# Both feed-forward down stages with seven half products, and operand sums made in the up stages

## The chip, the core and the metric

One core of a Trainium2 chip runs the whole layer. The metric is the device time of one execution in microseconds (us). TensorE (PE) multiplies, VectorE (DVE) and ScalarE (ACT) work on tiles, GpSimd (POOL) does tiny root computations and issues DMAs, SyncE (SP) issues most DMAs.

## What is computed

One layer for 2048 tokens of width 1024: a norm, a combined projection, attention and a time mixing, then a merge with `w_out`, a residual, and a feed-forward block with a residual:

```
m = sigmoid(gA) * (yA @ proj_a) + sigmoid(gB) * (yB @ proj_b)
x = x + RMSNorm_post(m @ w_out)
x = x + RMSNorm_post2(relu(RMSNorm_pre2(x) @ w_up)^2 @ w_down)
```

`w_up` is 1024x4096, `w_down` 4096x1024, all in float32. Each factor is split into a high and a low part (`split`, L72: a cast by ACT, a subtraction by DVE), and a product is three matmuls (`mm3`, L77).

## The kernel before

The tokens are four groups `g` of 512. For each group the kernel runs the time mixing, the attention and `phase_merge` (L987), whose last part is the output projection: 192 matmuls `ps_o`, after which ACT copies the result into the tiles `o` and they are stored to `od`. Under the projection of groups 1 and 2, `after` (L1070) runs the residual of the group before, one 128-token tile after the other (`residual_steps`, L1028): load `o` and `x`, mean square on ACT, root on POOL, two DVE steps that give the new `x` (stored to `x1`), a second mean square and root, one DVE step with the gain, eight transposes on PE (`ps_ht`), two copies `hf` on ACT and their stores to `ht`.

The feed-forward block works on two halves of two groups each: up, down, up, down. An up stage (`phase_up`, L1125) has 16 blocks `i`. A block multiplies a 256-column piece of `w_up` by the two groups with seven products of half size in place of eight, for which sums of the four quarters of the tokens (`t1` to `t4`, `b22`) and of the weights (`s1` to `s4`) are wanted. The first two products of a block need no sums; those of blocks 0 to 7 are made ahead, in the two PSUM banks of pool `pd`, and meanwhile `operands` makes the `t` tiles ready: it loads sums that `combinations` (L1095) has made earlier and stored in `td`, and splits them. The result goes through relu and square (`hidden`, L1184). ACT's copy is called `z`, DVE's first addition `r`.

The first down stage (`phase_down`, L1255) is plain: 32 blocks of 128 rows of `w_down`, two at a time, added into `u`. Beside it run the residuals of groups 2 and 3 (`residuals`, L1063), the `combinations` of the second half and the first operand of the second up stage (`first_half`). Its closing steps (`final`) norm `u`, add the residual and store `out`. The second down stage (`phase_down_sums`, L1327) takes 8 of the 32 blocks plainly and the other 24 in three batches of seven half products. For that the second up stage also stores sums of its hidden tiles (`differences`, L1201, on DVE, stores by POOL); there the square is made by ACT, in the first up stage by DVE with stores by POOL.

A recording layer decides where each instruction stands in its engine's order; each engine takes its own in that order.

## Time and profile before

| what | us |
|---|---|
| median of 3 runs | 3340.6 (3338.98 to 3341.16) |
| profiled execution | 3337.64 |
| its span, first to last instruction | 3335.9 |
| output projection of group 3 | 1987.33 to 2034.26 |
| first up stage | 2034.26 to 2340.18 |
| first down stage | 2340.18 to 2700.22 |
| second up stage | 2700.22 to 3009.26 |
| second down stage, to the last matmul | 3009.26 to 3326.22 |

The times of the stages are read in windows from the span's start. A row of windows gives each engine's busy time with its instruction count, then the clock that was granted to PE (1.00 is full), the DMA share and GB/s. Rows of a wait give the sum, the count and the longest.

### The profile page before, as it was taken

Reading aid. Unit: us, or ns where it says so; the run is one execution under the profiler, and the core shown is the slowest. Engines: PE = TensorE matmul, PEld = TensorE weight load, DVE = VectorE, ACT = ScalarE, POOL = GpSimd, SP = SyncE. Lnnn points to the kernel's source line nnn. Section 1 sums busy time; section 2 is a strip of 40 time slices with the busy share of each in tenths; the row PEclk is TensorE's granted clock in tenths of the full one; section 3 lists DMA queues with packets and bytes.
Section 4 is the critical chain, followed back from the end, with each engine's and each line's share of the span. In section 5 each row is a group of like instructions: output and inputs, shape, how many; then the busy total and the mean of one; then the engine's idle time right before and its main releaser. Section 6 shows DMA issues by size and latency. Waiting matters only on the chain. (4 is left out here: it accounts for less than half of the span.)

```text
span 3335.9 us, 49381 instructions
## 1 busy us (share of the span) xinstructions
PE 3244.5 (97%) x19089; PEld 2608.4 (78%) x19089; DVE 2284.0 (68%) x3814; ACT 1463.2 (44%) x2331; POOL 382.7 (11%) x732
## 2 busy tenths in 40 slices
PE   7999999999999999999999999999999999999998
PEld 6777787777777777777777777888888878888887
DVE  6774656765665774565774675877877787776788
ACT  4434634444644444644434644333431254454432
POOL 2210002111012210012210000111200011100000
PEclk9999999999999999999999999999999999999999
DMA  5224343125263224354224256434756364554444
GB/s 157 80 89 147 98 145 120 61 90 182 91 236 129 69 86 168 106 205 151 83 83 152 87 206 237 131 120 142 268 177 202 106 242 162 169 171 153 141 162 133
DMA packets 166099, 478.43 MB, mean 143 GB/s; under 512 B 17564, under 2 KB 34144, under 8 KB 163176
## 3 DMA queue, kind: packets, MB, share of 16 engines
q1 hardware_dynamic: 110004, 361.97, 32.9%
q0 software_dynamic: 18688, 63.98, 5.0%
q10 hardware_dynamic: 37172, 49.32, 4.1%
q8 instruction: 151, 2.47, 0.3%
q14 instruction: 84, 0.69, 0.1%
HBM read 355.64 MB, written 122.71 MB: 143 GB/s over the span
## 5 line engine op out<-in xcount | busy, mean ns | idle before, releaser
L83 PE MATMUL psd<-hh,whi 128*128 128x512 f32 x1344 | 542.5, 404 | 2.3 <-DVE QA L835 2.3
L83 PE MATMUL psd<-hl,whi 128*128 128x512 f32 x1344 | 539.3, 401 | 0.0
L83 PE MATMUL psd<-hh,wlo 128*128 128x512 f32 x1344 | 536.5, 399 | 0.0
L74 ACT CAST whi<-wraw 128x1024 fp32r<-128x1024 f32 x232 | 243.7, 1050 | 532.7 <-PE psd L83 421.9
L83 PE MATMUL ps_dn<-fop 128*128 128x512 f32 x1920 | 439.7, 390 | 2.1 <-DVE u L1291 1.5
L75 DVE TENSOR_TENSOR wlo<-wraw,whi 128x1024 fp32r<-128x1024 f32 x232 | 283.1, 1220 | 208.9 <-ACT whi L74 188.1
L83 PEld LDWEIGHTS ps_dn<-fop 128*128 128x128 f32 x1920 | 359.4, 188 | 78.6 <-DVE u L1291 2.3
L83 PEld LDWEIGHTS psd<-hh,whi 128*128 128x128 f32 x1344 | 256.1, 191 | 57.5 <-issue 3.4
L83 PEld LDWEIGHTS psd<-hh,wlo 128*128 128x128 f32 x1344 | 255.8, 190 | 54.1 <-issue 3.5
L83 PEld LDWEIGHTS psd<-hl,whi 128*128 128x128 f32 x1344 | 255.8, 190 | 50.8 <-issue 2.1
L83 PE MATMUL ps_dn<-fop,fop 128*128 128x512 f32 x1008 | 228.6, 389 | 0.0
L83 PEld LDWEIGHTS ps_dn<-fop,fop 128*128 128x128 f32 x1008 | 189.3, 188 | 39.2
L1291 DVE TENSOR_TENSOR u<-u,ps_dn 128x512 f32<-128x512 f32 x240 | 160.6, 683 | 54.3 <-PE ps_dn L83 53.8
L895 DVE CUSTOM_DVE_ANT_0 sc<-bias,ps_s 128x640 f32<-128x640 f32 (+4 forms) x128 | 94.1, 735 | 54.6 <-PE ps_s L889 50.6
L74 ACT CAST fop<-wdraw 128x1024 fp32r<-128x1024 f32 x40 | 41.9, 1047 | 191.8 <-DVE u L1291 88.7
L900 ACT ACTIVATE sc<-sc,mn 128x640 f32<-128x640 f32 (+4 forms) x128 | 97.8, 764 | 35.2 <-DVE mn L895 30.1
L74 ACT CAST s12h<-s 128x1024 fp32r<-128x1024 f32 x32 | 33.7, 1054 | 169.5 <-PE ps_u L83 169.5
L1019 PE MATMUL ps_o<-whi,mh 128*128 128x512 f32 x256 | 101.9, 398 | 1.9 <-ACT o L1025 1.9
L83 PE MATMUL ps_p<-yh,whi 128*128 128x512 f32 x256 | 102.1, 399 | 0.7 <-DVE th L985 0.7
L1019 PE MATMUL ps_o<-wlo,mh 128*128 128x512 f32 x256 | 101.8, 397 | 0.7 <-DVE wlo L75 0.7
L83 PE MATMUL ps_p<-yh,wlo 128*128 128x512 f32 x256 | 102.1, 399 | 0.0
L83 PE MATMUL ps_p<-yl,whi 128*128 128x512 f32 x256 | 101.5, 396 | 0.0
(378 smaller groups left out, 6741.8 us busy)
## 6 DMA issues: line engine op xcount, KB each, us to landing
wraw<-in_w_in_dram SPq DMA_DIRECT2D x168, 512.0 KB, 3.7
wraw<-in_w_up_dram SPq DMA_DIRECT2D x80, 512.0 KB, 4.5
ar<-sd SPq DMA_DIRECT2D x21, 1024.0 KB, 4.8
wdraw<-in_w_down_dram SPq DMA_DIRECT2D x40, 512.0 KB, 4.0
araw<-ad SPq DMA_DIRECT2D x40, 512.0 KB, 4.0
gd<-gate ACTq DMA_DIRECT2D x64, 256.0 KB, 2.3
wraw<-in_w_out_dram SPq DMA_DIRECT2D x32, 512.0 KB, 3.7
ad<-r POOLq DMA_DIRECT2D x64, 256.0 KB, 2.4
```

Of the source, the lines that this page charges most:

```text
L74: self.nc.scalar.copy(hi, src)
L75: self.nc.vector.tensor_tensor(lo, src, hi.bitcast(F32), ALU.subtract)
L83: mm = nc.tensor.matmul(ps, l, r, start=start and n == 0, stop=stop and n == last).ins
L895: nc.vector.tensor_tensor_reduce(sc[:, 0:n], bias[:, s0:640], pss[:, c0 : c0 + n], 1.0, 3.0e38, ALU.add, ALU.min, mn,)
L900: nc.scalar.activation(sc[:, 0:n], sc[:, 0:n], AF.Exp, scale=-1.0, bias=mn, accum_out=sm)
L1019: nc.tensor.matmul(ps[t], l[:, k, ts], r[:, k % 2], start=k == 0 and j == 0, stop=k == KB - 1 and j == 2)
L1291: nc.vector.tensor_tensor(u[t][:, ns], u[t][:, ns], ps, ALU.add)
```

## The change

- `phase_down_sums` becomes `phase_down` and serves both halves; the plain stage, `combinations`, `residuals` and `td` are gone. The first up stage makes the sums of its hidden tiles as the second does.
- `operands` loads the four quarters of the tokens from `ht` into free slots of the two 16 KB `z` tiles, in two passes; each pass makes four sums on DVE and then five splits. The second pass is loaded by POOL's queue into the same slots.
- The residual of group 2 moves under the output projection of group 3; that of group 3 follows it, from the tiles `o` without a trip to memory, beside the first products of the first up stage.
- A closing step of a tile (`final`) is queued behind the first half of the next tile. In the first half `out` is stored by POOL. Beside these steps, the weights of the first two blocks of the second up stage are loaded and split, and its first operand too (`nxt`).

```
-    def phase_merge(self, g, o, between, early=iter(())):
+    def phase_merge(self, g, o, between, pt, tp):
...
             advance(between)
+            if g == self.NG - 1:
+                rp = e(tc.tile_pool(name="mgr", bufs=2, reuse_waits="tile"))
+                res = [self.residual_steps(g, rp, pt, *self.gs, t, o[t]) for t in range(GT)]
+                for i in range(GT + 2):
+                    for t in (i - 2, i - 1, i):
+                        if 0 <= t < GT:
+                            advance(res[t], 1)
...
-        if 0 < g < 3:
-            gs = self.gains(sp, 3)
-            res = [self.residual_steps(g - 1, self.late, pt, *gs, t) for t in range(GT)]
+        if g > 0:
+            self.gs = self.gains(sp, 3 if g + 1 < self.NG else 2)
+            res = [self.residual_steps(g - 1, self.late, pt, *self.gs, t) for t in range(GT)]
...
             def operands():
-                td, g1 = self.td[half], self.ht[2 * half + 1]
-                for n, src in (
-                    ("t2", td[:, 3]), ("t3", td[:, 1]), ("t1", td[:, 0]), ("b22", g1[:, hi4]), ("t4", td[:, 2])
-                ):
-                    h, l = T[n]
-                    for k in (0, 2):
-                        ks = slice(k, k + 2)
-                        nc.sync.dma_start(l[:, ks].bitcast(F32), src[:, ks])
-                        self.split_here(h[:, ks], l[:, ks])
+                g0, g1 = self.ht[2 * half], self.ht[2 * half + 1]
+                t1, t3, b22, t4 = (slots[:, n : n + 2] for n in range(0, early, 2))
+                t2 = z[:, early - 2 : early]
+                for k in (0, 2):
+                    ks = slice(k, k + 2)
+                    for t, src in ((t1, g0[:, lo4]), (t3, g1[:, lo4]), (b22, g1[:, hi4]), (t4, g0[:, hi4])):
+                        (nc.gpsimd if k else nc.sync).dma_start(t, src[:, ks])
+                    for o, x, y in ((t1, t3, t1), (t2, b22, t1), (t3, b22, t3), (t4, t4, t2)):
+                        nc.vector.tensor_tensor(o, x, y, ALU.subtract)
+                    for n, src in (("t2", t2), *((("b22", b22), ("t4", t4), ("t3", t3)) if half else (("t3", t3), ("b22", b22), ("t4", t4))), ("t1", t1)):
+                        self.split(*(x[:, ks] for x in T[n]), src)
                         yield
...
             def summed(i):
-                return sums and FIRST <= i < FIRST + BATCHES * XB
+                return FIRST <= i < FIRST + BATCHES * XB
...
-                if not sums:
-                    nc.vector.tensor_tensor(out, out, out, ALU.mult)
-                    nc.gpsimd.dma_start(self.ad[fb][:, th], out)
-                    return
                 nc.scalar.activation(out, out, AF.Square)
...
             for i in range(early):
-                A11, A12 = parts(load(2 * i), ("a1", "s12", "s3")[i % 3], KB)
+                A11, A12 = made.pop(i, None) or self.up_first(i, load, parts)
...
-                for n, queue in enumerate((nc.sync, nc.scalar)):
+                for n, queue in enumerate((nc.gpsimd, nc.gpsimd) if follow else (nc.sync, nc.scalar)):
...
-                        keep(y[th][:, t, n * H : (n + 1) * H], ps, False)
+                        kept = keep(y[th][:, t, n * H : (n + 1) * H], ps, False)
                         halve(th, t, n, gt, scaled, ssq)
-                    final(th, t, fp, scaled, ssq)
+                        if n == 0 and at:
+                            with tc.issue_after(kept):
+                                final(*done)
+                            advance(beside, 1)
+                    done = th, t, fp, scaled, ssq
+            final(*done)
...
+            def nxt(loaded):
+                bp = bpool(ahead, "b1", side="right")
+                self.sp = bpool(ahead, "ops1", side="right")
+                load, parts = self.up_raw(rp), self.up_parts(self.sp)
+                for i in range(2):
+                    self.made[i] = self.up_first(i, load, parts)
+                return self.first_half(2, bp, loaded)
...
-            self.phase_up(0, zp, rp, cb, pn, 8)
-            self.phase_down(0, zp, rp, cb, pn, beside)
-            self.phase_up(1, zp, rp, cb, pn, 8, True)
-            self.phase_down_sums(1, zp, bp, rp, cb, pn)
+                with ExitStack() as u:
+                    self.phase_up(0, zp, rp, cb, pn, bpool(u, "ops", side="right"), 8, {})
+                self.phase_down(0, zp, bp, rp, cb, pn, nxt)
+            self.phase_up(1, zp, rp, cb, pn, self.sp, 8, self.made)
+            ahead.close()
+            self.phase_down(1, zp, bpool(ctx, "b2"), rp, cb, pn)
```

PE, start of the first down stage, before (`fop` are split blocks, `o_prev` normed tiles of a residual):

```order
L83 MATMUL ps_u<-t4h,s3l 128x512
L83 MATMUL ps_dn<-fop 128x512 x82
L1054 MATMUL ps_ht<-ident,o_prev 128x128 x8
L83 MATMUL ps_dn<-fop 128x512 x25
L1054 MATMUL ps_ht<-ident,o_prev 128x128 x8
```

PE at the same place after the change:

```order
L83 MATMUL ps_u<-t4h,s3l 128x512
L83 MATMUL ps_dn<-fop 128x512 x48
L83 MATMUL ps_dn<-fop_22026 128x512 x48
L83 MATMUL ps_dn<-fop_22115 128x512 x3
```

PE among the early products of the first up stage after the change (`o_18802` and `o_18803` are tiles 2 and 3 of group 3):

```order
L83 MATMUL ps_u<-bh,s3l 128x512
L1060 MATMUL ps_ht<-ident,o_18802 128x128 x8
L83 MATMUL ps_u<-bh,s3h 128x512
L83 MATMUL ps_u<-bl,s3h 128x512
...
L1060 MATMUL ps_ht<-ident,o_18803 128x128 x8
```

The transposes have left the first down stage; those of group 3 stand among the early products of the first up stage.

DVE, start of the first up stage, before (`r` takes a product from PSUM, the others are low parts of splits):

```order
L1189 TENSOR_TENSOR r<-z,ps_u 128x512
L75 TENSOR_TENSOR a1l<-wraw,a1h 128x1024
L1192 TENSOR_TENSOR r<-r 128x512
L1114 TENSOR_TENSOR t2l<-t2l,t2h 128x1024
L1189 TENSOR_TENSOR r<-z,ps_u 128x512
L75 TENSOR_TENSOR s12l<-wraw,s12h 128x1024
L1192 TENSOR_TENSOR r<-r 128x512
L1114 TENSOR_TENSOR t2l<-t2l,t2h 128x1024
L1114 TENSOR_TENSOR t3l<-t3l,t3h 128x1024
L1189 TENSOR_TENSOR r<-z,ps_u 128x512
```

DVE there after the change, from the last residual to the first pass's splits:

```order
L1046 SCALAR_TENSOR_TENSOR o_18804<-o_18804,rs_p,g_post_mix 128x1024
L1047 TENSOR_TENSOR xr<-xr,o_18804 128x1024
L1182 TENSOR_TENSOR r<-z,ps_u 128x512
L1054 SCALAR_TENSOR_TENSOR o_18804<-xr,rs_r,g_pre_ffn 128x1024
L1182 TENSOR_TENSOR r<-z,ps_u 128x512
L1214 TENSOR_TENSOR s_19947<-wraw 128x512
L75 TENSOR_TENSOR a1l<-wraw,a1h 128x1024
L75 TENSOR_TENSOR t2l<-z,t2h 128x1024
L75 TENSOR_TENSOR t3l<-slots,t3h 128x1024
L75 TENSOR_TENSOR b22l<-slots,b22h 128x1024
L75 TENSOR_TENSOR t4l<-slots,t4h 128x1024
```

DVE a little later, the second pass up to the first full block (`slots` and `z` on the left are sums, `r` belongs to blocks 6 and 7):

```order
L1155 TENSOR_TENSOR slots<-slots 128x1024
L75 TENSOR_TENSOR s4l<-s_19948,s4h 128x512
L1155 TENSOR_TENSOR z<-slots 128x1024
L1155 TENSOR_TENSOR slots<-slots 128x1024
L1155 TENSOR_TENSOR slots<-slots,z 128x1024
L75 TENSOR_TENSOR t2l<-z,t2h 128x1024
L75 TENSOR_TENSOR t3l<-slots,t3h 128x1024
L75 TENSOR_TENSOR t4l<-slots,t4h 128x1024
L1182 TENSOR_TENSOR r<-z,ps_u 128x512
L75 TENSOR_TENSOR t1l<-slots,t1h 128x1024
L1182 TENSOR_TENSOR r<-z,ps_u 128x512
L75 TENSOR_TENSOR s12l<-s_19947,s12h 128x1024
```

Where one `r` stood behind two or three splits, the `r` of blocks 3 and 4 now stand behind residual steps and those of blocks 6 and 7 behind the sums and splits of the second pass.

## The prediction

> **What bounds the kernel now.** I read the page's table of busy times first, then the windows of the stages, the two groups of the down stages' matmuls and TensorE's waits in each window. PE is TensorE, DVE VectorE, ACT ScalarE.

> ```profile
> PE 3244.5 (97%) x19089; PEld 2608.4 (78%) x19089; DVE 2284.0 (68%) x3814; ACT 1463.2 (44%) x2331; POOL 382.7 (11%) x732
> core 0: us, PE busy (x) PEld busy (x) DVE busy (x) ACT busy (x) POOL busy (x), PEclk, DMA share, GB/s
> 1475.80:1532.50 56.70, 53.15 (x258) 42.47 (x257) 33.65 (x32) 30.48 (x48) 11.78 (x26) 1.00 0.69 230
> 1987.33:2034.26 46.93, 44.76 (x194) 35.73 (x192) 23.43 (x23) 18.43 (x22) 0.71 (x1) 1.00 0.64 239
> 2034.26:2340.18 305.92, 304.96 (x1346) 252.17 (x1344) 227.38 (x313) 116.37 (x156) 33.71 (x63) 1.00 0.45 151
> 2340.18:2700.22 360.04, 357.85 (x1607) 295.73 (x1606) 288.55 (x377) 102.95 (x145) 37.05 (x73) 1.00 0.57 188
> 2700.22:3009.26 309.04, 305.12 (x1339) 250.76 (x1339) 232.98 (x315) 159.31 (x225) 30.25 (x54) 1.00 0.55 189
> 3009.26:3326.22 316.96, 316.41 (x1393) 260.92 (x1391) 243.49 (x291) 119.05 (x155) 6.74 (x21) 1.00 0.43 147
> ```

> The rows are the output projection of group 2's merge, that of group 3, then up, down, up, down of the two halves; what remains to 3335.9 is the tail. PE is busy 97% of the span and nearly all of every stage: time goes where matmuls go, and a stall has to be added to that. The first down stage takes 360.04 us, the second, which already works with seven products, 316.96.

> ```profile
> L83 PE MATMUL ps_dn<-fop 128*128 128x512 f32 x1920 | 439.7, 390 | 2.1 <-DVE u L1291 1.5
> L83 PE MATMUL ps_dn<-fop,fop 128*128 128x512 f32 x1008 | 228.6, 389 | 0.0
> ```

> One 128x512 matmul occupies PE for 439.7/1920 = 0.229 us (228.6/1008 = 0.227; the mean of 390 ns overlaps its neighbour). Up stages have 1344 of them. The 1339 of the second up window tell that five already ran in the down window ahead of it (5 x 0.229 = 1.1 us).

> **The change part by part.** First down stage. Plain, it has 32 blocks x 8 x 2 x 3 = 1536 matmuls; with sums 8 blocks x 48 + 3 x 7 x 48 = 1392. So 144 go, 33.0 us at 0.229. Its 64 transposes for the residuals of groups 2 and 3 and their waits go too. The whole is read at once from the twin: 360.04 - 1.1 - 316.96 = **42.0 us less**. DVE is no new bound there: 243.49 of 316.96 us in the twin, and the closing steps get seven more split subtractions (two ahead of the seam, four of the first operand, one late), some 8 us, in a last stretch that PE fills for 192 x 0.229 = 44 us; I count that covered, 0 to 3 us.

> Residuals of group 2 move under group 3's output projection. Group 2's projection in the first window does the same work for group 1, and another 32 transposes besides.

> ```profile
> PE ps_ht L1054 <- DVE o_prev L1048: 3.3, 4, 1.1
> ```

> In that window PE waits 3.3 us for the four tiles. 56.70 - 192 x 0.229 - 3.3 = 9.4 us for 64 transposes, so 4.7 for 32. Without those of the norm the stage takes 52.0, against 46.93 now: **+5.1**, up to 7 if the small waits of today's window stay.

> Residuals of group 3 and all operand sums move to the start of the first up stage. This is the part to work out. Today the first full block there starts at 2078.9, 44.6 us after the projection:

> ```profile
> L83 PE MATMUL ps_u<-t2h,s12h x128: 389/389/501, 2078.9 to 2997.7; 128*128 128x512 f32 x128
> 2048.29 1.22 DVE L1114 TENSOR_TENSOR t2l<-t2l,t2h 128x1024 fp32r<-128x1024 f32 x1
> 2049.42 1.22 DVE L1114 TENSOR_TENSOR t3l<-t3l,t3h 128x1024 fp32r<-128x1024 f32 x1
> 2059.50 0.68 DVE L1192 TENSOR_TENSOR r<-r 128x512 f32<-128x512 f32 x1
> 2060.10 1.22 DVE L1114 TENSOR_TENSOR t4l<-t4l,t4h 128x1024 fp32r<-128x1024 f32 x1
> 2047.02 0.63 ACT L1190 ACTIVATE r<-r 128x512 f32<-128x512 f32 x1
> 2047.55 1.04 ACT L1113 CAST t3h<-t3l 128x1024 fp32r<-128x1024 f32 x1
> 2048.49 0.58 ACT L1213 COPY z<-ps_u 128x512 f32<-128x512 f32 x1
> L1040 DVE SCALAR_TENSOR_TENSOR o_prev<-o_prev,rs_p,g_post_mix x16: 1273/1284/1289, 972.8 to 2464.8; 128x1024 f32<-128x1024 f32 x16
> L1038 ACT ACTIVATE sqo<-o_prev x16: 1052/1059/1062, 970.4 to 2460.8; 128x1024 f32<-128x1024 f32 x16
> L130 POOL TENSOR_TENSOR rs_r<-rs_v,nhalf x64: 549/558/1519, 9.4 to 3330.2; 128x1 f32<-128x1 f32 x64
> L133 POOL TENSOR_SCALAR rs_p<-rs_r x16: 226/229/1023, 972.5 to 2463.0; 128x1 f32<-128x1 f32 x16
> L1057 ACTq DMA_DIRECT2D ht<-hf x32: 366/410/1049, 980.2 to 2503.7; - x32
> ht<-hf ACTq DMA_DIRECT2D x32, 256.0 KB, 6.7
> ```

> Back to back, DVE takes 1.14 us for 128x1024 and 0.60 for 128x512, ACT 0.94 for a cast, 0.53 and 0.48 for halves and 0.4 for each DMA it issues; a mean square needs 1.1 us on ACT and about 1.25 on POOL before DVE may go on. Both engines take their instructions in the written order. Each early block has two products in the two banks of pool `pd`: the first product of block i+1 needs `z` of block i copied by ACT, the second needs `r` of block i added by DVE. So every `r` that stands late in DVE's order holds PE.

> I follow the new order by hand, in us from the end of the projection. DVE can begin at 3.1 (copy of `o`, its square, its root). Ahead of `r` of block 1 stand `r` of block 0 and 12 rows of 128x1024 (two and a half residuals, one split, four sums): 12 x 1.14 + 2 x 0.6 = 14.9, with some 2 us of waits for roots, so it is read at 20; PE, with its transposes, wanted that bank at 16.5. `r` of block 2 follows its matmuls at 23.6; then six rows, `r` of block 3 and some 5 us of waits for the roots of tiles 3 and 4 bring `r` of block 4 to 36.7 (PE alone would be there at 31.5). Now nine operand splits, three weight splits, four sums and seven halves stand up to and with `r` of block 6: 16 x 1.14 + 7 x 0.6 = 22.4, with a wait for a load **60 us**, and ACT likewise copies `z` of block 6 behind the casts of the same operands, at about 57.7, its hf copies for tile 4 having waited for a store (6.7 us to land, two buffers). PE has finished block 6 at 49.6 and stands still for 8 us; block 7 ends at 57.7 + 24 x 0.229 = 63.2, and the cast of the next `s12` adds 1.3, with the store's wait about 66. That is 66 - 44.6 = 21 us. Without any wait on DVE, `r` of block 4 would be through at 3.1 + 19 x 1.14 + 5 x 0.6 = 28, `r` of block 6 at 50, the first `t2` product at 55: 11 us. I take **+20**, nearer to the chain with its waits, since these follow from the written order; 11 and 25 are the ends. What these steps put on queues is in it: eight stores of `ht` and seven of hidden tiles on ACT (15 x 0.4 = 6 us of its order), the stores of `x1` on POOL ahead of the next root.

> After 8 us of standing PE may lose its clock. The trace has such places in the recurrence:

> ```profile
> PE ps_t L596 <- DVE X L575: 6.7, 2, 3.8
> 614.00:621.50 7.50, 4.89 (x22) 1.00 0.28 90
> 621.50:628.30 6.80, 6.58 (x75) 0.50 0.15 58
> ```

> A wait of up to 3.8 us is followed by 6.80 us at half the clock, which costs up to 3.4 us; I take **+2**, since part of it falls into time when DVE is late anyway. [...]

> Sums of hidden tiles in the first up stage (squares to ACT, differences on DVE, as the second up stage has them) and the second up stage's own start:

> ```profile
> PE ps_u L83 <- ACT z L1213: 1.7, 2, 1.1
> PE ps_u L83 <- ACT s12h L74: 0.9, 1, 0.9
> PE ps_u L83 <- DVE s3l L75: 0.5, 1, 0.5
> PE ps_u L83 <- DVE s12l L75: 0.4, 1, 0.4
> PE ps_u L83 <- ACT s3h L74: 0.3, 1, 0.3
> ```

> The first two are the waits of the second up stage up to 2760, the others after. The later 1.2 us come with the differences: **+1.2** in the first up stage. The 2.6 at the start belong to the seam. There the sums now cost DVE 8 x 1.14 = 9 us more, while the first half's four splits and two weight splits (7 us) were done earlier. Followed in the same way, `r` of blocks 1 and 4 hold PE 0.8 and 1.1 us and the cast of `s12` 1.4: 3.3, **+0.7**, between -2 and +6. Loads of the second operand halves go through POOL, queued behind the closing stores of the half before and, in the first half, behind POOL's roots; DVE is busy until after they land, so 0 while that cover holds.

> Tail. Today the last addition waits behind two closing steps of the tile before:

> ```profile
> 3328.05 0.68 DVE L1378 TENSOR_TENSOR y<-y,ps_dn 128x512 f32<-128x512 f32 x1
> ```

> The last matmul ends at 3326.2 (end of the last window); with those steps moved up, the addition can start at about 3326.6: **-1.4**. In the first half the stores of `out` go through POOL, where the next tile's root stands behind them; it is wanted a tile (24 x 0.229 = 5.5 us) later, so nothing.

> Sum: -42.0 + 5.1 + 20 + 2 + 1.2 + 0.7 - 1.4 = -14.4. The profiled execution took 3337.64 us, 3.0 below the median of 3340.6, so 3323 for it and **3326 us** for a median.

> **The rivals.** Cover holds: DVE's waits at the start of the first up stage vanish and its block of splits costs the floor of 11 us, without a lost clock and with nothing at the seam. -42.0 + 5.1 + 11 + 1.2 - 1.4 = -26: 3314. For it: ACT stands at 44% and DVE at 68% overall. Against: both are in order, and the residuals' roots interleave with the splits.

> Given back: the first up stage loses 25, the seam 6, the closing steps 3, the projection 7, clock 3.4. -42.0 + 25 + 6 + 3 + 7 + 1.2 + 3.4 - 1.4 = +2, less what cannot all happen; I give it as -6: 3335, no change that a measurement tells.

> Slower: the second operand loads can be issued only as the first halves' splits give their slots back, one after another through POOL. Today's operand loads at that place land slowly:

> ```profile
> t3l<-td SPq DMA_DIRECT2D x2, 512.0 KB, 9.6
> ```

> If four such loads were to follow one another at 9.6 us, the last would land 38 us after the first release at 40, and the sums behind it would start at 78 instead of 50: 27 us more in the first up stage and, released 19 us in, some 20 in the second. That gives 3326 + 47 = 3373. It decides from the point where both stages together lose 22 us more than forecast. Against it: such loads overlap today, since the ninth of ten is already split at 2060.10, 26 us after the projection.

> That no product is saved is excluded by the order of the program, which has 2784 matmuls of `ps_dn` in place of 2928.

> **How the numbers follow.** The forecast has 0.56, the covered case 0.20, given back 0.19, slower 0.05. A difference under 0.2% (6.7 us) can't be told from none. The forecast's own range is 3318 to 3335 (11 to 25 us in its largest term, the seam's ends). All of the covered case and the forecast is faster but for 0.02; of the given-back case a quarter is. Faster 0.79, same 0.16, slower 0.05. The range of 3311 to 3337 leaves out the slower case and the tails of the others.

> **What would show it.** Right: the first down stage takes 317 us and has no transposes; group 3's projection takes 52; in the first up stage the first `t2` product starts some 66 us after the projection, PE's longest wait there is about 8 us on `z` or `r` of block 6, and the clock dips behind it; the second up stage starts as now. Wrong: a first down stage over 325 us, waits on operand loads at either start, or no wait over 3 us in the first up stage.

## The result, and the profile after

The changed kernel takes 3377.2 us (median of three executions, 3375.3 to 3382.8), against 3340.4 for the kernel before: the ratio is 1.0115, with a 95% interval of 1.0097 to 1.0133. It was forecast at 3326 and is slower. A fourth execution took 8476 us and is left out; with it the median is the 3380.0 that the expectations below start from. The profiled execution took 3375.31 us, with a span of 3373.5, which is 37.6 more than the span before.

The first view is the table of busy times and then the windows of the stages, in the same columns as before: the projection of group 3, first up, first down, second up, second down, and the tail after the last matmul.

```profile
PE 3240.2 (96%) x18945; PEld 2587.3 (77%) x18945; DVE 2276.9 (67%) x3742; ACT 1554.9 (46%) x2463; POOL 385.3 (11%) x732
1985.62:2040.52 54.90, 49.66 (x225) 40.17 (x224) 33.16 (x29) 30.23 (x44) 11.66 (x24) 0.97 0.78 271
2040.52:2387.10 346.58, 323.61 (x1378) 258.22 (x1377) 249.20 (x323) 172.62 (x247) 43.23 (x76) 0.98 0.51 174
2387.10:2712.50 325.40, 319.67 (x1393) 262.81 (x1392) 246.84 (x292) 124.91 (x160) 13.41 (x29) 0.99 0.44 156
2712.50:3034.20 321.70, 314.71 (x1346) 252.66 (x1345) 235.38 (x316) 155.58 (x221) 33.41 (x64) 0.99 0.51 174
3034.20:3357.50 323.30, 318.32 (x1393) 261.86 (x1391) 249.94 (x296) 123.42 (x160) 5.79 (x18) 0.99 0.41 144
3357.50:3373.50 16.00, 0.04 (x1) 0.00 (x0) 5.28 (x8) 1.45 (x4) 1.87 (x6) 0.60 0.30 112
```

PE issues 144 instructions fewer and is busy almost as long, 3240.2 us against 3244.5. So 28.7 of the 33.0 us of removed products came back as time in which PE counts as busy, which no list of waits shows. The second column of the up stages shows where most of it is: the first one is busy for 323.6 us instead of 305.0. It has the same 1344 products, 32 transposes more, and stretches at half the clock (0.98 in the mean). The table sets the terms of the sum against the spans of the stages:

| term | forecast | measured |
|---|---|---|
| first down stage | -42.0 | -33.5 |
| projection of group 3 | +5.1 | +8.0 |
| first up stage (start 20, clock 2, sums 1.2) | +23.2 | +40.7 |
| second up stage (the seam) | +0.7 | +11.6 |
| second down stage | 0 | +6.3 |
| tail | -1.4 | +6.3 |
| all ahead of that projection | 0 | -1.7 |
| sum | -14.4 | +37.7 |

**Matmuls without a gap, and slower.** The next view is one window in the last part of the first up stage, where PE is never idle and its clock is full: first the kernel before, then the changed one.

```profile
2110.00:2330.00 220.00, 220.00 (x973) 182.15 (x972) 166.31 (x235) 79.23 (x106) 25.76 (x48) 1.00 0.40 130
```

```profile
2210.00:2380.00 170.00, 170.00 (x730) 137.00 (x729) 122.14 (x167) 85.50 (x119) 17.29 (x32) 1.00 0.48 163
```

220.00/973 is 0.226 us a matmul, 170.00/730 is 0.233. From one matmul's start to the next the trace has 0.2267 us before and 0.2333 after, in every product of the first up stage and in those with `t` and `b22` operands in the second; the first-half products there and the down stages stay between 0.2267 and 0.2284. That is 6.6 ns x 1344 = 8.9 us in the first up stage and 6.6 x 960 = 6.3 in the second. One matmul by itself is shown as 389 ns in the first of these windows and as 393 to 398 ns in the second; it overlaps its neighbour, so what it costs is read from the starts, or from busy time over count.

**The start of the first up stage.** PE's longer waits from the projection's end to the first `t2` product, which starts at 2115.42, 74.9 us after it (44.6 before); the second row is the transposes of the moved residual:

```profile
PE ps_u L83 <- ACT z L1202: 14.7, 3, 12.6
PE ps_ht L1060 <- DVE o L1054: 5.4, 4, 3.1
```

Around the longest, ACT's order in time; the bracket is the idle time ahead of an instruction and what ended it:

```profile
2080.53 0.59 ACT L1202 COPY z<-ps_u 128x512 f32<-128x512 f32 x1 [1.10 <-issue]
2081.01 1.06 ACT L74 CAST a1h<-wraw 128x1024 fp32r<-128x1024 f32 x1
2081.96 1.05 ACT L74 CAST t2h<-z 128x1024 fp32r<-128x1024 f32 x1
...
2094.56 1.04 ACT L74 CAST b22h<-slots 128x1024 fp32r<-128x1024 f32 x1 [2.87 <-DMA slots<-ht]
...
2102.25 1.04 ACT L74 CAST t2h<-z 128x1024 fp32r<-128x1024 f32 x1 [0.69 <-DVE z L1155]
2103.38 1.05 ACT L74 CAST t3h<-slots 128x1024 fp32r<-128x1024 f32 x1
2104.52 1.04 ACT L74 CAST t4h<-slots 128x1024 fp32r<-128x1024 f32 x1
2105.71 0.59 ACT L1202 COPY z<-ps_u 128x512 f32<-128x512 f32 x1
```

The last row is `z` of block 6, for which PE stands. It is queued behind the casts of the second operand pass, as forecast, but that pass is later than forecast: its first load is issued by POOL at 2086.89 and its first cast runs at 2094.56, with ACT idle for it. The two rows `t2h<-z` show one thing more. The raw sum `t2` lies in the last two slots of the tile `z`, where `z` of blocks 6 and 7 has to go. PE then gets half the clock for four times 3.4 us:

```profile
2097.80:2111.50 13.70, 5.15 (x12) 4.09 (x13) 10.57 (x11) 6.03 (x7) 0.00 (x0) 0.50 0.28 82
```

Most of that falls into the time in which PE stands anyway: it is busy for 5.15 us of the 13.70, so half the clock costs about 2.6 us there.

**The closing steps.** DVE's and PE's waits in the last 28 us of the first down stage:

```profile
DVE scaled L1361 <- DMA out_dram<-scaled: 11.8, 5, 3.8
PE ps_dn L83 <- DVE y L1297: 5.2, 1, 5.2
```

DVE stands for the store of the tile `scaled` two tiles earlier. The same wait, 4.5 us in five pieces, stands in the second half's closing steps, so that DVE is late at the very end:

```profile
3360.52 0.69 DVE L1361 TENSOR_TENSOR scaled<-y,g_post 128x512 f32<-128x512 f32 x1 [1.08 <-DMA out_dram<-scaled]
3361.13 0.74 DVE L1371 SCALAR_TENSOR_TENSOR scaled<-scaled,rs_r,x1r 128x512 f32<-128x512 f32 x1
3361.79 0.68 DVE L1297 TENSOR_TENSOR y<-y,ps_dn 128x512 f32<-128x512 f32 x1
```

The last addition starts 4.3 us after the last matmul's end (3357.5); before, it was 1.8.

**The second down stage.** Some 30 us into it PE waits 4.0 us on `y`. DVE's order in front of the additions that free the PSUM banks:

```profile
3058.16 1.22 DVE L75 TENSOR_TENSOR fop<-araw,fop 128x1024 fp32r<-128x1024 f32 x1
3059.30 2.35 DVE L1320 TENSOR_TENSOR qt<-qb,qb 128x1024 f32<-128x1024 f32 x2
3061.57 1.22 DVE L75 TENSOR_TENSOR fop<-ar,fop 128x1024 fp32r<-128x1024 f32 x1
...
3064.97 1.22 DVE L75 TENSOR_TENSOR fop<-qt,fop 128x1024 fp32r<-128x1024 f32 x1
3066.11 2.47 DVE L1297 TENSOR_TENSOR y<-y,ps_dn 128x512 f32<-128x512 f32 x4
```

### The profile page after: what moved, and what is told of

It reads as the page before. It is cut to its first block, busy times and chain, and to the rows that moved or that the text cites. A ratio compares the mean times of both kernels' runs of the same rounds, so it can differ in the third digit from the quotient of the medians.

```text
span 3373.5 us, 48976 instructions
## 1 busy us (share of the span) xinstructions
PE 3240.2 (96%) x18945; PEld 2587.3 (77%) x18945; DVE 2276.9 (67%) x3742; ACT 1554.9 (46%) x2463; POOL 385.3 (11%) x732
## 5 line engine op out<-in xcount | busy, mean ns | idle before, releaser
L83 PE MATMUL psd<-hh,whi 128*128 128x512 f32 x1344 | 541.6, 403 | 2.3 <-DVE QA L834 2.3
L83 PE MATMUL psd<-hl,whi 128*128 128x512 f32 x1344 | 538.5, 401 | 0.0
L83 PE MATMUL psd<-hh,wlo 128*128 128x512 f32 x1344 | 535.5, 398 | 0.0
L74 ACT CAST whi<-wraw 128x1024 fp32r<-128x1024 f32 x232 | 243.6, 1050 | 522.9 <-PE psd L83 422.7
L83 PE MATMUL ps_dn<-fop,fop 128*128 128x512 f32 x2016 | 457.3, 389 | 0.0
L83 PEld LDWEIGHTS ps_dn<-fop,fop 128*128 128x128 f32 x2016 | 378.4, 188 | 78.6
L75 DVE TENSOR_TENSOR wlo<-wraw,whi 128x1024 fp32r<-128x1024 f32 x232 | 283.1, 1220 | 203.0 <-ACT whi L74 183.5
L83 PEld LDWEIGHTS psd<-hh,whi 128*128 128x128 f32 x1344 | 255.4, 190 | 57.6 <-issue 3.4
L83 PEld LDWEIGHTS psd<-hh,wlo 128*128 128x128 f32 x1344 | 255.2, 190 | 54.2 <-issue 3.5
L83 PEld LDWEIGHTS psd<-hl,whi 128*128 128x128 f32 x1344 | 255.2, 190 | 50.7 <-issue 2.1
L83 PE MATMUL ps_dn<-fop 128*128 128x512 f32 x768 | 181.6, 398 | 10.7 <-DVE y L1297 9.7
L74 ACT CAST fop<-ar 128x1024 fp32r<-128x1024 f32 x84 | 87.6, 1048 | 213.5 <-PE ps_dn L83 166.5
L83 PEld LDWEIGHTS ps_dn<-fop 128*128 128x128 f32 x768 | 146.5, 192 | 45.2 <-DVE y L1297 11.8
L1297 DVE TENSOR_TENSOR y<-y,ps_dn 128x512 f32<-128x512 f32 x168 | 109.8, 681 | 48.0 <-PE ps_dn L83 47.7
L75 DVE TENSOR_TENSOR fop<-ar,fop 128x1024 fp32r<-128x1024 f32 x84 | 102.3, 1220 | 48.2 <-ACT fop L74 48.2
L74 ACT CAST s12h<-s 128x1024 fp32r<-128x1024 f32 x32 | 33.5, 1048 | 163.9 <-PE ps_u L83 163.9
L1196 POOL DMA_DIRECT2D sd<-slots x96 | 51.9, 541 | 472.9 <-DVE slots L1195 467.5
L83 PE MATMUL ps_p<-yh,whi 128*128 128x512 f32 x256 | 102.0, 398 | 1.5 <-DVE th L984 1.5
## 6 DMA issues: line engine op xcount, KB each, us to landing
wraw<-in_w_in_dram SPq DMA_DIRECT2D x168, 512.0 KB, 3.6
wraw<-in_w_up_dram SPq DMA_DIRECT2D x80, 512.0 KB, 4.3
sd<-slots POOLq DMA_DIRECT2D x96, 256.0 KB, 4.5
gd<-gate ACTq DMA_DIRECT2D x64, 256.0 KB, 2.3
wraw<-in_w_out_dram SPq DMA_DIRECT2D x32, 512.0 KB, 6.3
sd<-slots ACTq DMA_DIRECT2D x60, 256.0 KB, 2.9
```

The source lines that it names most:

```text
L74: self.nc.scalar.copy(hi, src)
L75: self.nc.vector.tensor_tensor(lo, src, hi.bitcast(F32), ALU.subtract)
L83: mm = nc.tensor.matmul(ps, l, r, start=start and n == 0, stop=stop and n == last).ins
L1196: nc.gpsimd.dma_start(place(i, "s3" if o == "a21" else o), R[o])
L1297: return nc.vector.tensor_tensor(dst, dst, ps, ALU.add).ins
```

## The experiments

The theory after the result has four separate causes: the start addresses of the operands (matmuls 3% slower in the up stages), the chain at the start of the first up stage, the two `scaled` buffers, and the order at the second down stage. Rivals stand with each run. Stages are compared within profiled executions, one for each kernel, since the part ahead of group 3's projection ends anywhere from 1982.7 to 1990.3 us whatever is edited behind it. Stages differ between these traces by 1 to 4 us without a known reason: in the changed kernel and variants whose edits don't aim at it, the second down stage takes 323.3 to 324.3 us, the second up stage without the padding 321.6 to 325.2.

### Where operands start

The change moved the weight pool `ops` of the up stages from the left side of SBUF to the right. The built programs place the moving operands `b` and `t` at byte 672, counted modulo 1024, in both kernels, the weights at 672 before and at 992 after. (In the changed kernel's second up stage `b` too lies on the right, at 992.)

`pad_right`, on the changed kernel:

```
+            e(tc.tile_pool(name="pad", bufs=1, side="right")).tile([P, 80], F32, name="pad")
             rp = e(tc.tile_pool(name="raw", bufs=4, side="right", reuse_waits="tile"))
```

> The changed kernel with 320 unused bytes per partition ahead of the pools on the right side of SBUF, so that the weights of the up stages start at the same remainder of 1024 bytes as the moving operands on the left (672 and 672, instead of 992 and 672). Nothing else differs. Start theory (a matmul is slower when its two operands start at different remainders): both up stages go back from 0.2333 to 0.2267 us from one matmul's start to the next, 1344 x 0.0066 = 8.9 us per stage; the time falls by 16 to 18 us, to about 3363. Side theory (slower because weights and moving operand lie on different sides): no change, 3380. Traffic theory (slower because of the stores and loads that the change put beside the products): no change either.

Measured: 3366.7 us, ratio 1.0066 [1.0049, 1.0082]. The first row is the window in the first up stage again, the second one in the second; the third is the changed kernel in the second:

```profile
2210.00:2380.00 170.00, 170.00 (x751) 140.77 (x750) 124.45 (x170) 86.58 (x120) 17.36 (x32) 1.00 0.50 169
2860.00:3020.00 160.00, 160.00 (x708) 132.53 (x707) 113.61 (x159) 78.67 (x111) 17.34 (x32) 1.00 0.50 169
2870.00:3030.00 160.00, 160.00 (x692) 129.26 (x692) 107.93 (x149) 75.03 (x106) 15.69 (x29) 1.00 0.47 162
```

170.00/751 = 0.2264: the period is back at 0.2267 though the two operands still lie on different sides, amid the same traffic. Side and traffic theories fall. The first up stage gained 7.5 us (339.1); the second only 0.7 (321.0), because there its start takes 55.9 us to the first `t2` product instead of 52.5 and PE waits 1.9 us for `s12l` later. That the faster matmuls bring the longer start isn't shown: `zzbb` below, with slow ones, takes 55.0 us to that product, and `all_fixes`, with fast ones, 52.8. The expected 8.9 for that stage was too much in any case, since its first-half products had not been slow.

`pad_left_before`, on the kernel before:

```
+            e(tc.tile_pool(name="pad", bufs=1)).tile([P, 80], F32, name="pad")
             sp = e(tc.tile_pool(name="ops", bufs=1, reuse_waits="tile"))
```

> The kernel before with 320 unused bytes ahead of its weight pool of the up stages, on the same side as all else. Start theory: both up stages go from 0.2267 to 0.2333 us per matmul, and the time rises by 16 to 18 us, to about 3358. Side theory and traffic theory: no change, 3340.

Measured: 3362.85 us, 21 more than before, in one run. The first up stage takes 314.8 us instead of 305.9 and the second 325.4 instead of 315.8 (from its first `ps_u` in each), and all products read 0.2333.

```profile
2120.00:2340.00 220.00, 220.00 (x945) 177.25 (x944) 162.63 (x228) 78.31 (x105) 24.94 (x46) 1.00 0.39 126
```

Same side, nothing of the change in it, 945 matmuls in 220 us instead of 973: 0.233 us each instead of 0.226. In this run the start addresses alone do it.

`ladder_before`, on the kernel before (32 bytes ahead of `t1`, then 32, 64 and 384 ahead of the weights `s12`, `s3` and `s4`):

```
+                if n == "t1":
+                    tb.tile([P, 8], F32, name="pad" + n)
...
+                if tag in pads:
+                    sp.tile([P, pads.pop(tag)], F32, name="pad" + tag)
...
+            pads = {"s12": 8, "s3": 16, "s4": 96}
```

> The kernel before with small unused tiles, so that weights start off from the moving operand by 32 bytes (first-half products, and the product with t1), 64 (t2), 128 (t3 and t4) and 512 (b22), modulo 1024. Start theory: whichever of these offsets still reads 0.2267 us per matmul tells the modulus that matters; if only equality modulo 1024 counts, all six products read 0.2333 and the time is about 3357; if 32 or 64 bytes are the unit, all stay at 0.2267 and the time is 3340. Side theory and traffic theory: no change in any product.

Measured: 3356.8 us. First and last matmul of the `t2` product (64 off, 11 steps) and, of the `b22` product (512 off), the fourth and the eighth after it:

```profile
2161.75 0.39 PE L83 MATMUL ps_u<-b22h,s4h 128*128 128x512 f32 x1
...
2163.56 0.40 PE L83 MATMUL ps_u<-b22h,s4l 128*128 128x512 f32 x1
...
2166.59 0.39 PE L83 MATMUL ps_u<-t2h,s12h 128*128 128x512 f32 x1
...
2169.16 0.39 PE L83 MATMUL ps_u<-t2h,s12l 128*128 128x512 f32 x1
```

(2169.16 - 2166.59)/11 = 0.234 and (2163.56 - 2161.75)/8 = 0.226. Offsets of 32, 64 and 128 are slow (means 0.2323 to 0.2333), 512 is not: the first three steps of that product still take 0.23, the others 0.226, and the mean of all is 0.228. So in this run the unit is 512 bytes or less, and more than 128.

`pad256_before` (as `pad_left_before`, with 64 floats instead of 80):

> The kernel before with 256 unused bytes ahead of the weight pool of the up stages, so that every weight starts 256 bytes off from its moving operand. If the unit is 512 bytes, all products of both up stages read 0.2333 us per matmul and the time is about 3358; if it is 256 bytes, they stay at 0.2267 us and the time at 3341.

Measured: 3341.1 us, one run; up stages 305.9 and 315.8, as before.

```profile
2120.00:2330.00 210.00, 210.00 (x928) 173.96 (x927) 160.27 (x226) 76.67 (x103) 24.83 (x46) 1.00 0.40 131
```

210.00/928 = 0.2263. So the remainder of the start address modulo 256 bytes sorts all offsets tried: 320, 64, 32 and 128 off are slow (0.2323 to 0.2333), 256 and 512 are not (0.2263 and 0.228).

`aligned_before` uses this elsewhere, on the kernel before:

```
+        self.yctx.enter_context(tc.tile_pool(name="pad1", bufs=1, side="right")).tile([P, 88], F32, name="pad1")
         yp = self.yctx.enter_context(tc.tile_pool(name="ya", bufs=1, side="right", reuse_waits="tile"))
...
+            e(tc.tile_pool(name="pad2", bufs=1)).tile([P, 32], F32, name="pad2")
             pp = e(tc.tile_pool(name="atp", bufs=1, reuse_waits="tile"))
...
+            if g + 1 < self.NG:
+                cp.tile([P, 32], F32, name="pad3")
             mh = cp.tile([P, KB, G], F32R, name="mh")
```

> The kernel before with three unused pieces (352, 128 and 128 bytes) so that the projections' operands too start at the same remainder of 512 bytes: y of proj_a and proj_b (512 and 32 before, against 672 of the weights) and mh, ml of the merges of groups 0 to 2 (32 against 672). Nothing else differs. Start theory with a unit of 512 bytes: ps_p goes from 0.233 to 0.227 us per matmul (4 x 192 matmuls, 4.8 us) and ps_o of groups 0 to 2 from 0.2324 to 0.227 (3 x 192, 3.1 us); time 3333, 0.2% faster. If the 512 bytes of the earlier run were chance or the rule holds only in the up stages: 3341, no change.

Measured: 3337.7 us, ratio 0.9987 [0.9978, 0.9996]. `ps_p` went from 0.2330 to 0.2280 us a matmul, `ps_o` of groups 0 to 2 from 0.2324 to 0.2278, about 6 us by the counts; the interval excludes no change, barely. In `ps_p` it is the moving operand that was shifted while the weights stayed, so here too the difference of the two starts counts and not the weights' place. Group 3's `ps_o` had always read 0.2275, with `mh` at 672: the trace of before had held the hint.

### The closing steps

`scaled4`, on the changed kernel:

```
-                    scaled = fp.tile([P, D], F32, tag="scaled", name="scaled")
+                    scaled = fp.tile([P, D], F32, tag="scaled", bufs=4, name="scaled")
```

> The changed kernel with four buffers in place of two for the tile in which the last rows of a down stage are scaled and stored. Store theory (VectorE waits for the store of the tile two before, 1 to 3.8 us per tile, since the closing step of a tile is now written half a tile later and stores through the GpSimd queue): the waits for out_dram ahead of scaled vanish, the first down stage loses its 5.2 us wait and the half clock behind it, 6 to 9 us, and the tail shrinks from 16.0 us to 9 or 10; together 12 to 15 us, to about 3366. Rival (the closing steps are late for the root on GpSimd or the load of x1, and another wait takes the place): under 4 us.

Measured: 3368.1 us, ratio 1.0075 [1.0059, 1.0092]. First down stage and tail:

```profile
2386.20:2704.50 318.30, 317.39 (x1393) 260.75 (x1392) 247.14 (x293) 124.81 (x161) 15.93 (x29) 1.00 0.45 160
3351.60:3363.50 11.90, 0.00 (x0) 0.00 (x0) 2.79 (x4) 0.72 (x2) 0.94 (x3) 0.66 0.20 73
```

The store waits are gone, the stage gains 7.1 us and the tail 4.1. The last addition now starts at 3351.62, as soon as the last matmul is done. That the tail is 11.9 and not below 9.7 has another reason, below.

### The start of the first up stage

`t2_qw`, on the changed kernel (the split of `t2` follows in halves):

```
-                t2 = z[:, early - 2 : early]
...
+                    t2 = [up.tile([P, G], F32, tag=n, name=n) for n in "qw"]
```

> The changed kernel with the raw t2 sum in the tiles q and w, which are free until the first full block, in place of the last two slots of the tile z. So z of blocks 6 and 7 need not wait until t2 of the second pass is split. Slot theory (the 12.6 us wait for z of block 6 comes from that slot): the longest wait falls under 6 us, the first t2 product comes 4 to 8 us earlier than 74.9 and the time falls by 4 to 8 us, to about 3374. Chain theory (the splits themselves are late, whatever z does): the wait moves to block 7 or to the t2 product and the time changes by under 3 us.

Measured: 3374.2 us, ratio 1.0094 [1.0079, 1.0109]. The first `t2` product comes 66.9 us after the projection, the stage takes 339.7 us, 6.9 less. PE's waits there, to set against the 12.6:

```profile
PE ps_u L83 <- ACT z L1208: 6.9, 3, 3.7
PE ps_u L83 <- DVE r L1188: 2.2, 2, 1.8
```

The slot theory holds; it says nothing on why the rest is still 22 us later than before.

`late_residual`, on the changed kernel (the new generator computes what `residual_steps` did, out of `od`, in the tile `z`):

```
-            if g == self.NG - 1:
-                rp = e(tc.tile_pool(name="mgr", bufs=2, reuse_waits="tile"))
-                res = [self.residual_steps(g, rp, pt, *self.gs, t, o[t]) for t in range(GT)]
...
+                if i == early and half == 0:
+                    late = self.residual_late(zp, cb, up, pt)
...
+                advance(late, 2)
```

> The changed kernel with the residual of group 3 taken out of the start of the first up stage: the tiles o are stored to memory like those of the other groups, and the residual's four tiles run beside blocks 8 to 15 of that stage, in the 16 KB tile z that is free from block 8 on; all of the computation is still done. Chain theory (the first t2 product comes 74.9 us after the projection because the residual's steps on VectorE and ScalarE, and the memory that they hold, which b22, t4 and t1 need, keep the operand splits back): the first t2 product comes 48 to 58 us after it, no wait over 4 us is left there, the half clock of 13.7 us goes, and the first up stage shrinks from 346.6 to 320 to 330 us, since its transposes stay; time about 3358. Load theory (the second pass of operand loads through GpSimd's queue sets the end): the t2 product stays later than 68 us and the time falls by under 8 us.

Measured: 3360.4 us, ratio 1.0055 [1.0040, 1.0070]. The first `t2` product comes 56.7 us after the projection, and the stage takes 330.7 us.

```profile
PE ps_u L83 <- ACT z L1236: 4.9, 2, 3.7
PE ps_u L83 <- DVE r L1216: 1.7, 1, 1.7
```

15.9 us of the stage's 40.7 hang on the residual standing at its start; the load theory falls, since the second pass is loaded by POOL here too. The stage is just over the expected 330. Whether the splits were late because of the residual's instructions in the engines' orders, or because its tiles hold memory that `t4`, `b22` and `t1` take over, this run doesn't tell apart, and it wasn't tried.

### The second down stage

`fetch_early`, on the changed kernel:

```
             w2 = load(2, True)
+            fetch(0, ("b12", "b11", "b22", "b21"))
             plain([w1], False)
             w3 = load(3, False)
-            with tc.issue_after(self.loaded):
-                fetch(0, ("b12", "b11", "b22", "b21"))
```

> The changed kernel with the first load of the w_down quarters of a down stage issued where the kernel before issued it, ahead of the second plain block's products and not behind the fourth block's load. Order theory (these loads land late, so the sums and splits made of them stand in VectorE's order right ahead of four additions that free PSUM banks): the gap of 4.4 us some 30 us into the second down stage shrinks to 1 or 2 us and its half clock goes; that stage goes from 323.4 to 318 to 320 us and the time falls by 3 to 6 us, to about 3375. Rival (the four splits still stand ahead of those additions, whenever the loads land): the gap stays at 3.5 us or more, no change in the time.

Measured: 3373.85 us, ratio 1.0104 [1.0085, 1.0123], not distinguishable from the changed kernel. The stage takes 323.3 us, and PE's wait is the same to a tenth:

```profile
PE ps_dn L83 <- DVE y L1297: 4.0, 1, 4.0
```

The order theory falls and its rival holds: the splits stand ahead of those additions whenever the quarters are fetched.

`zzbb`, on the changed kernel:

```
-            w0, w1 = load(0, False), load(1, True)
+            w0, w1 = load(0, False), load(1, False)
...
-            w3 = load(3, False)
+            w3 = load(3, True)
```

> The changed kernel with the first four plain blocks of a down stage split into the tiles z, z, b, b in place of z, b, z, b; the second block then need not wait for a b tile. In the changed kernel the b tiles of the second down stage lie on the memory of t4 and b22 of the up stage before, whose last reader is the last product there. Memory theory (VectorE's and ScalarE's work for the second block is late for that reason and piles up until the additions that free PSUM banks stand 4.4 us too late): the gap some 30 us into the second down stage falls under 1.5 us, the stage goes from 323.4 to 317 to 319 us, the time falls by 4 to 6 us, to about 3375. Order theory (the planner puts the splits for the first half product ahead of those additions whatever comes before): the gap stays over 3 us, the time within 2 us of 3380.

Measured: 3375.75 us, ratio 1.0100 [1.0086, 1.0114]. The stage takes 321.1 us, the wait is halved:

```profile
PE ps_dn L83 <- DVE y L1297: 2.5, 2, 2.0
```

Between the two expectations: 2.2 of the stage's 6.3 us seem to hang on which tile the second block's operands get. That is twice what traces differ by there, and `best` below, with the same edit, has 320.1 against the 324.2 of `all_fixes`. The rest of that stage's loss stays open.

### All together

`all_fixes` has the padding, four buffers, the early fetch and the late residual.

> The changed kernel with the 320 unused bytes, the four scaled buffers, the early load of the quarters and the late residual, all at once. If the four causes are separate and the whole explanation, the sum of their parts is -13 (padding, measured), -12 (buffers, measured), -4 and -22: 3380 - 51 = 3329, faster than the kernel before by 0.3%. If the waits only move from place to place, it stays above 3340.

Measured: 3337.8 us, ratio 0.9990 [0.9981, 0.9999]; first up 324.7, first down 318.9, second up 316.0, second down 324.2, tail 11.4. Each stage shows its own edits: the first up stage -21.9 us (15.9 and 7.5 when tried singly), the first down stage -6.5 (7.1), the second up stage -5.7, the tail -4.6. The stages of that execution take 38 us less than the changed kernel's, but the part ahead of the projection took 4 us more, and the gain from the early fetch that the expectation counted doesn't exist.

`best` adds `t2_qw`, `zzbb`, the padding of `aligned_before`, and one step of delay for the transposes under the last projection:

```
+        lag = 2 if nrm else 3
+        for i in range(GT + lag):
+            for t in (i - lag, i - 1, i):
```

> The changed kernel with padding, four scaled buffers, early load of the quarters, late residual, raw t2 in q and w, z, z, b, b, the transposes of the residual of group 2 one step later under the last projection, and the three unused pieces of the projections. If the terms add: 3337.8 (measured with the first four) - 5 for z, z, b, b - 4 for q and w - 4 for the transposes - 8 for the projections = 3317, faster than the kernel before by 0.7%. If the later ones only move waits, 3325 to 3330.

Measured: 3327.2 us, ratio 0.9951 [0.9939, 0.9964]: faster than both kernels, by less than the terms added up to. Its stages, in the order of the first table:

```profile
1982.70:2039.60 56.90, 51.68 (x225) 41.52 (x224) 33.17 (x28) 29.99 (x45) 11.52 (x24) 0.94 0.76 259
2039.60:2358.20 318.60, 311.25 (x1377) 254.78 (x1377) 246.26 (x329) 173.37 (x266) 41.20 (x84) 1.00 0.61 208
2358.20:2676.10 317.90, 316.97 (x1393) 260.81 (x1392) 247.75 (x293) 124.65 (x159) 15.31 (x29) 1.00 0.46 162
2676.10:2991.30 315.20, 306.83 (x1346) 251.67 (x1345) 235.93 (x324) 158.10 (x225) 33.63 (x64) 1.00 0.52 177
2991.30:3311.40 320.10, 317.23 (x1393) 260.58 (x1391) 250.14 (x297) 122.50 (x160) 7.02 (x21) 1.00 0.43 149
3311.40:3322.80 11.40, 0.00 (x0) 0.00 (x0) 2.79 (x4) 0.72 (x2) 0.93 (x3) 0.63 0.21 77
```

The delay of the transposes was a miss: the projection takes 56.9 us instead of 54.4, since PE now waits 2.0 us for `o` and 0.9 us for a split, and 1.9 us still for a tile of the residual. The loss of that stage isn't explained.

## Why the prediction was wrong, point by point

The sum left two costs out, a lower speed of the products themselves and too few buffers for the moved closing steps, and its largest term, the start of the first up stage, was too small.

- **"Time goes where matmuls go."** The step took 0.229 us for any 128x512 matmul and left the up stages' 1344 products out of the sum, as if they couldn't change. They did, by 8.9 and 6.3 us by their starts; the padding alone brought the ratio from 1.0115 to 1.0066, about 16 us, with some 8 us of uncertainty. None of the rivals had this. The pool's new side was part of the change, and the prediction made nothing of it.
- **First down stage, -42.0.** The size was right: with four `scaled` buffers it is 318.3 - 358.9 = -40.6. What failed is "I count that covered, 0 to 3 us" for the closing steps. The cost of the splits was worked out, but not the wait of the moved `final` for its buffer: half a tile later, with the store half a tile later too, two buffers don't last (7.1 us).
- **First up start, +20 and clock +2.** The mechanism was named rightly, PE standing for `z` of block 6 behind the second pass, and the size was off: `t2` product at 74.9 us instead of 66, 12.6 us of standing instead of 8. 8.0 of it is the slot of `t2` in the tile `z`, which made `z` wait for a split and not only stand behind casts in ACT's order. Without that slot the product comes at 66.9 us, but that this is the forecast is in part luck: PE's longest wait on `z` is then 3.7 us, not 8. The waits that were forecast for `r` of blocks 1 and 4 (3.5 and 5.2 us) did not show; PE waited 5.4 us for the tiles of its transposes. Half the clock lasted 13.7 us instead of 6.8 but cost about 2.6 us there, not far from the +2; another 3.4 us of it, from 2060.3 on, came behind a wait for one of these tiles. "0 while that cover holds" for POOL's loads: it didn't hold, ACT stood idle 2.87 us for them and DVE 1.3. What that cost was not measured by itself. The "slower" rival built on it (four loads after one another, 38 us) did not happen: they were issued within 3.2 us.
- **Seam, +0.7 between -2 and +6.** Without the 6.3 us of slower matmuls the second up stage lost 5.3, inside the bounds.
- **Second down stage, not in the sum.** Its code was taken as the same, so 317.0 was kept. It lost 6.3 us: some 2.2 hang on the second block's `b` tile, which now lies on memory that the last product of the up stage reads; the rest is open.
- **Tail, -1.4.** The store waits cost 4.1 us (`scaled4`); without them the last addition starts with the last matmul's end, as forecast. The other part is the DRAIN with which GpSimd closes the program, which comes with its last root (3363.88 and 3363.92 us). The first row is the kernel before, the second the changed one; the three numbers are the shortest, the middle and the longest of three in ns, and the longest is the one that starts first:

```profile
L1603 POOLq DRAIN  x3: 40/93/1582, 3330.1 to 3335.3; - x3
L1541 POOLq DRAIN  x3: 40/93/8526, 3363.9 to 3373.2; - x3
```

  SyncE's last drain comes at 3368.25 us, and GpSimd, from 3363.88 on in this DRAIN, answers it only at 3372.75, 4.5 us later; before, it answered within 0.03. From the end of DVE's last closing step (`scaled`) to the end of the span it is 3.7 us before, 7.6 in the changed kernel, 7.7 in `scaled4` and 7.3 in `best`. Why the DRAIN takes 8.53 us instead of 1.58 stays open; the number of DMAs that GpSimd issues is 192 in both kernels.
- **Projection, +5.1.** +8.0 measured; the bound was 7. PE waits 4.8 us for the residual's tiles where the model stage had 3.3, and half the clock for 3.41 us behind the longest of these waits (0.97 in the window) costs some 1.7 us; together that is about the difference to the forecast.

The range failed because it was built from the terms of the written order alone. Of the missing 52 us (37.6 + 14.4), 15 are an effect of addresses, 11 are buffers that became too few when steps moved in time, and 7 are the slot of `t2` (what the stage gained in `t2_qw`); the rest is the second down stage, GpSimd's late answer, the seam and the projection.

## What to carry to other kernels

When a change moves a pool that feeds matmuls like these, compare the start addresses of both operands modulo 256 bytes before and after; here 128 to 352 unused bytes put it right, and busy time over count in a window without idle time shows it (0.226 against 0.233 us). A step that is moved later keeps its buffers longer: count the buffers of everything that it stores. An operand parked in a tile that is written next is a wait like any other, and neither the order of instructions nor the diff's arithmetic shows it: list for each tile its last reader and its next writer.

## What the runs showed of the hardware that was not expected

```profile
2715.61:2719.03 3.42, 2.56 (x12) 1.00 0.73 255
2719.03:2722.44 3.41, 1.77 (x8) 1.00 1.01 345
2722.44:2725.86 3.42, 3.42 (x17) 1.00 1.02 406
2729.27:2732.68 3.41, 1.37 (x6) 1.00 0.07 24
2732.68:2736.10 3.42, 3.42 (x10) 0.50 0.45 94
```

  An idle gap of 2.5 us that ends at 2720.7 is cut in two by a boundary, and no half clock follows. One of 2.1 us that ends at 2731.3 lies nearly whole in one stretch, 60% of which is idle, and half the clock follows from 2732.68 on. In the traces of the two kernels, from 20 us to the last matmul, each stretch at full clock that is idle for more than 57% is followed by one at half the clock, and none that is idle for less than 41%; of the seven between, two are (42 and 43% idle) and five are not (43 to 56%). What decides there isn't shown.
- One matmul in a stream is recorded as 389 ns long where it follows the one before after 0.2267 us (kernel before, 2110 to 2330), and as 393 to 398 ns where it follows after 0.2333 (changed kernel, 2210 to 2380).
- GpSimd's closing DRAIN takes 8.53 us in the trace of the changed kernel and 1.58 in that of the kernel before. No run here shows why.
